# Eight experts on one core: TensorE's addresses in bytes, and the two copying engines in a loop of four turns

## The chip, the core and the metric

The kernel runs on one core of a Trainium2 chip. Its engines work side by side and meet only at semaphores: TensorE (PE in the profile, with its weight loads as PEld), VectorE (DVE), ScalarE (ACT), GpSimd (POOL) and SyncE (SP). The last two issue most of the transfers here, POOL on one queue and SP on another; sixteen DMA engines carry them out. The metric is the time of one execution on the device, in microseconds; lower is better.

## The reference

```python
n_experts, capacity, hidden, expert_hidden = 8, 256, 512, 2048
def reference(x, w1, w2):          # x [8,256,512], w1 [8,512,2048], w2 [8,2048,512], all float32
    h = np.matmul(x, w1)
    h = np.maximum(h, 0)
    return np.matmul(h, w2).astype(np.float32)
```

Each of the eight experts has its own x, w1 and w2. The weights are 8 x 2 x 4.19 MB, x and the result 4.19 MB each.

## The kernel before

**Transfers.** POOL loads the weights, one transfer per expert and layer (`load_w1`, L129; `load_w2`, L132), which turns float32 into bfloat16 on the way, so 4.19 MB are read and 2.10 MB written. There are two buffers for w1 (the halves of `w1_sb`) and two for w2 (`w2_sb`), used by even and odd experts. The order on POOL is fixed: the second half of x (`x_c`, L140), w1 of experts 0 and 1, a unit matrix, w2 of 0 and 1, and then for each further pair the two w1 and the two w2 (L156 to L162). Before a w1, POOL waits until TensorE is through layer 1 of the expert that had the buffer (`s_h`, L158); before a w2, until TensorE is through layer 2 of that expert (`s_o`, L161). w2 of the last expert comes in two pieces, 9 and 7 sixteenths (`CUT`, L137 and L138). Behind all loads POOL issues the results of experts 0 to 3 as one transfer (L164). SP loads the first half of x (`x_f`, L90) and at the end issues the results of experts 4 to 6 (L124) and 7 (L126).

**Tokens.** In between SP serves as TensorE's usher: it waits for each load, in the order in which TensorE needs them, and raises `t_w` (L114, L119, L121, L122), which TensorE takes down again. Ahead of the second expert of a pair it also waits until the first one's result has left `pt_o` (L117, `copied`).

**x.** The tokens have to be transposed. ScalarE and VectorE each run four rounds of `take_x` (L180), one for odd and one for even experts (in the last two rounds, for halves of the rows that four experts share): `cast` (L170, the copy at L175) writes the tile `x_b` in bfloat16, TensorE transposes it in eight blocks (L243), and a copy (L191 or L194) takes it from `pt_tr` to `xe`.

**The layers.** TensorE runs a loop over four pairs of experts (L246). Layer 1 of both experts (L247): in four turns of 16 matmuls, half of each turn into `pt_h0`, half into `pt_h1`; it takes the weights with a step of 16 columns. VectorE applies the relu to every `pt_h0` (L224), ScalarE to every `pt_h1` (L207), both into `ht_sb`; `t_hb` and `t_ha` give the halves back. Then layer 2 of both experts (L268): 32 matmuls into the two halves of `pt_o`, in groups (`GRP`). ScalarE copies the whole of `pt_o` to `out_sb` for experts 0 to 5 (L211); for experts 6 and 7 (`SOLO`) ScalarE and VectorE copy a half each (L214, L228). TensorE's loops address their operands through registers; `ahead` (L232) works the addresses out before the matmuls that use them, in elements of the tile. ScalarE's and VectorE's instructions are written out for all eight experts.

Of the kernel before, what the change touches and what calls it, by code (L numbers as in the profile page):

```python
# [9 lines left out]
def kernel(  # L10
# [7 lines left out]
    nc = tc.nc  # L18
    P = 128
    bf = mybir.dt.bfloat16  # L20
    f32 = mybir.dt.float32
    relu = mybir.ActivationFunctionType.Relu

    E, C, H = x.shape
    F = w1.shape[2]
    MT = C // P
    KT1 = H // P
    KT2 = F // P
    FB = 4
    NQ = KT2 // FB  # L30
    G = E // 2
    CUT = 9
    GRP = {0: 2, 2: 4, 6: 5, 11: 5}
    SOLO = E - 2

    w1_r = w1.rearrange("e (p kt) n -> e p kt n", p=P)
    w2_r = w2.rearrange("e (p kt) n -> e p kt n", p=P)
# [10 lines left out]
    x_c = nc.alloc_sbuf_tensor("x_c", [P, J, H], bf)  # L48
    x_b = nc.alloc_sbuf_tensor("x_b", [P, 2, KT1 * MT, P], bf)
    xe = nc.alloc_sbuf_tensor("xe", [P, E * KT1 * C], bf)  # L50
    w1_sb = nc.alloc_sbuf_tensor("w1_sb", [P, 2 * KT1 * F], bf)
    w2_sb = nc.alloc_sbuf_tensor("w2_sb", [P, 2 * KT2 * H], bf)
    ht = nc.alloc_sbuf_tensor("ht_sb", [P, 2 * KT2, H], bf)
    ht_f = ht[:].rearrange("p k n -> p (k n)")
    w1_k = w1_sb[:].rearrange("p (k n) -> p k n", n=F)
    w2_k = w2_sb[:].rearrange("p (k n) -> p k n", n=H)
    o_sb = nc.alloc_sbuf_tensor("out_sb", [P, E, MT, H], f32)
    identity = nc.alloc_sbuf_tensor("identity", [P, P], bf)
    ph = [nc.alloc_psum_tensor(f"pt_h{b}", [P, FB // 2, C], f32) for b in range(2)]
    po = nc.alloc_psum_tensor("pt_o", [P, MT, H], f32)  # L60
    pt = [nc.alloc_psum_tensor(f"pt_tr{b}", [P, KT1 * MT, P], bf) for b in range(2)]

    sem = nc.alloc_semaphore
# [2 lines left out]
    s_out = [sem(f"s_out{i}") for i in range(3)]  # L66
    s_w1 = [sem(f"s_w1_{e}") for e in range(E)]
    s_w2 = [sem(f"s_w2_{e}") for e in range(E)]
    s_w2b = sem("s_w2b")
    s_id = sem("s_id")  # L70
    s_act = sem("s_act")
    s_dve = sem("s_dve")
    s_tr = sem("s_tr")
    s_h = sem("s_h")
    s_o = sem("s_o")
    t_xb = sem("t_xb")
    s_xe = [sem(f"s_xe{b}") for b in range(2)]
    t_w = sem("t_w")
    t_ha = sem("t_ha")
    t_hb = sem("t_hb")  # L80

    sp, pool, act, dve, pe = nc.sync, nc.gpsimd, nc.scalar, nc.vector, nc.tensor

    def take(s, n=1):
        pe.wait_ge(s, n).then_inc(s, -n)  # L85
# [11 lines left out]

    def copied(eng, n):
        eng.wait_ge(s_act, n)
        if n > SOLO:  # L100
            eng.wait_ge(s_dve, n - SOLO)


    for e in range(G // 2, G):
# [1 line left out]
    for e in range(0, E, 2):  # L106
        for b in range(2):

            if e < G:
                sp.wait_ge(s_xe[b], e // 2 + 1)  # L110
            elif e + b == G:
                for s in s_xe:
                    sp.wait_ge(s, G)
            sp.wait_ge(s_w1[e + b], 16).then_inc(t_w, 1)  # L114
        for b in range(2):
            if b:
                copied(sp, e + 1)  # L117
            if e + b < E - 1:
                sp.wait_ge(s_w2[e + b], 16).then_inc(t_w, 2)  # L119
            else:  # L120
                sp.wait_ge(s_w2[e + b], 16).then_inc(t_w, 1)  # L121
                sp.wait_ge(s_w2b, 16).then_inc(t_w, 1)  # L122
    copied(sp, E - 1)
    sp.dma_start(out_r[:, G:E - 1], o_sb[:, G:E - 1]).then_inc(s_out[1], 16)  # L124
    copied(sp, E)
    sp.dma_start(out_r[:, E - 1], o_sb[:, E - 1]).then_inc(s_out[2], 16)  # L126


    def load_w1(e):  # L129
        pool.dma_start(w1_k[:, e % 2 * KT1:(e % 2 + 1) * KT1], w1_r[e]).then_inc(s_w1[e], 16)  # L130

    def load_w2(e):  # L132
        k = e % 2 * KT2
        if e < E - 1:
            pool.dma_start(w2_k[:, k:k + KT2], w2_r[e]).then_inc(s_w2[e], 16)  # L135
        else:
            pool.dma_start(w2_k[:, k:k + CUT], w2_r[e, :, :CUT]).then_inc(s_w2[e], 16)  # L137
            pool.dma_start(w2_k[:, k + CUT:k + KT2], w2_r[e, :, CUT:]).then_inc(s_w2b, 16)  # L138

    pool.dma_start(x_c[:], x_rows).then_inc(s_xc, 16)  # L140
    load_w1(0)
# [10 lines left out]
        channel_multiplier=1,  # L152
    ).then_inc(s_id, 1)
    load_w2(0)
    load_w2(1)
    for e in range(2, E, 2):  # L156
        for b in range(2):
            pool.wait_ge(s_h, 2 * NQ * (e + b - 1))  # L158
            load_w1(e + b)
        for b in range(2):  # L160
            pool.wait_ge(s_o, MT * (e + b - 1))  # L161
            load_w2(e + b)  # L162
    copied(pool, G)
    pool.dma_start(out_r[:, :G], o_sb[:, :G]).then_inc(s_out[0], 16)  # L164
# [5 lines left out]
    def cast(eng, r, b):  # L170

        a = 2 * r + b
        src = x_f[:, a] if a < G else x_c[:, MT * (a - G):MT * (a - G + 1)]
        copy = act.copy if eng is act else dve.tensor_copy
        copy(  # L175
            x_b[:, b].rearrange("p (t m) q -> p m q t", m=MT),
            src.rearrange("p m (q t) -> p m q t", t=KT1),
        ).then_inc(t_xb, 1)

    def take_x(eng, b):  # L180
# [16 lines left out]
                ).then_inc(s_xe[b], 1)  # L197


    act.sem_inc(t_ha, 1)  # L200
    take_x(act, 1)
    for e in range(0, E, 2):
        for b in range(2):
            for q in range(NQ):
                act.wait_ge(s_h, 2 * (NQ * (e + b) + q) + 2)
                k = KT2 * b + FB * q + FB // 2
                act.activation(ht[:, k:k + FB // 2, :C], ph[1][:], relu).then_inc(t_ha, 1)  # L207
        for b in range(2):
            if e + b < SOLO:
                act.wait_ge(s_o, MT * (e + b + 1))  # L210
                act.copy(o_sb[:, e + b], po[:]).then_inc(s_act, 1)  # L211
            else:
                act.wait_ge(s_o, MT * (e + b) + 2)
                act.copy(o_sb[:, e + b, 1], po[:, 1]).then_inc(s_act, 1)  # L214


    dve.sem_inc(t_hb, 1)
    take_x(dve, 0)
    for e in range(0, E, 2):
        for b in range(2):  # L220
            for q in range(NQ):
                dve.wait_ge(s_h, 2 * (NQ * (e + b) + q) + 1)
                k = KT2 * b + FB * q
                dve.tensor_relu(ht[:, k:k + FB // 2, :C], ph[0][:]).then_inc(t_hb, 1)  # L224
        for b in range(2):
            if e + b >= SOLO:
                dve.wait_ge(s_o, MT * (e + b) + 1)
                dve.tensor_copy(o_sb[:, e + b, 0], po[:, 0]).then_inc(s_dve, 1)  # L228

    def ahead(flat, weights, first, places, n, step=1):  # L232
        aps = [flat[:, bass.ds(first + k, n, step=step)] for k in places]
        for ap in aps:
            pe.lower_ap(ap, for_matmul_weights=weights)
        return aps

    pe.wait_ge(s_id, 2)
    with pe.Fori(0, G) as _r:
        take(t_xb, 2)  # L240
        for b in range(2):
            for j in range(KT1 * MT):
                ins = pe.transpose(pt[b][:, j], x_b[:, b, j], identity[:])  # L243
            ins.then_inc(s_tr, 1)

    with pe.Fori(0, G) as g:  # L246
        with pe.Fori(0, 2) as b:  # L247
            xs = ahead(xe, False, (g * 2 + b) * (KT1 * C), [kt * C for kt in range(KT1)], C)
            take(t_w)
            with pe.Fori(0, NQ) as q:  # L250
                for i in range(FB):
                    if i % 2 == 0:
                        ws = ahead(
                            w1_sb, True, b * (KT1 * F) + q * FB,
                            [kt * F + i + j for j in range(2) for kt in range(KT1)], P, KT2,
                        )
                        take((t_hb, t_ha)[i // 2])
                    for kt in range(KT1):
                        ins = pe.matmul(  # L259
                            ph[i // 2][:, i % 2, :],  # L260
                            ws[i % 2 * KT1 + kt],
                            xs[kt],
                            start=(kt == 0),
                            stop=(kt == KT1 - 1),
                        )
                    if i % 2:
                        ins.then_inc(s_h, 1)
        with pe.Fori(0, 2) as b:  # L268
            for kt in range(KT2):
                if kt in GRP:  # L270
                    k0, ks = kt, range(kt, kt + GRP[kt])
                    ws = ahead(w2_sb, False, b * (KT2 * H), [k * H for k in ks], H)
                    hs = ahead(
                        ht_f, True, b * (KT2 * H), [k * H + m * P for k in ks for m in range(MT)], P
                    )
                if kt == 3 * FB:
                    pe.wait_ge(t_hb, 1)
                if kt in (0, CUT):
                    take(t_w)
                for m in range(MT):  # L280
                    ins = pe.matmul(  # L281
                        po[:, m],
                        hs[(kt - k0) * MT + m],
                        ws[kt - k0],
                        start=(kt == 0),
                        stop=(kt == KT2 - 1),
                    )
                    if kt == KT2 - 1:
                        ins.then_inc(s_o, 1)

    for s in s_out:
        sp.wait_ge(s, 16)
# [30 lines left out]
```

## Time and profile before

| | us |
|---|---|
| three runs: lowest, median, highest | 180.07, 180.76, 182.46 |
| the profiled execution | 180.42 |
| its span, from the first to the last instruction | 178.8 |
| busy: PE, PEld | 126.0, 87.1 |
| busy: ACT, DVE, POOL | 54.1, 40.9, 14.3 |
| 15 of the loads of weights, median from issue to landing | 25.1 |

The span is what the views of the profile show; the 1.6 us between it and the execution's time lie around it. A group's row reads: line, engine, operation, output from input, shapes, count, then busy time, mean nanoseconds of one, idle time of the engine just ahead of them and what ended it. A row of the timeline begins with the start and the length in us; the bracket is the idle time before. "issue" and "PEq" stand for the engine's own instruction stream. SPq is SP's queue. A row of stretches has the stretch, its length, each engine's busy time with the count, the clock granted to TensorE, the DMA engines' busy share and the GB/s that they wrote.

### The profile page before, as it was taken

The numbers are of one execution on the slowest core, as the hardware profiler recorded it, in microseconds if no ns is written. First come the engines' busy times: TensorE is split into PE (matmuls) and PEld (weight loads), VectorE is DVE, ScalarE is ACT, GpSimd is POOL, SyncE is SP. The second block draws the span as 40 slices with busy tenths as digits, with TensorE's granted clock in tenths as the row PEclk, the third lists the DMA queues.
The fourth block names the chain that finished last, engine by engine and source line by source line (L and its number), as shares of the span: only waits on it lengthen the run. The fifth ranks groups of instructions, "written<-read, shape, count | busy, mean of one in ns | idle before, by whom it ended". The sixth has DMA issues, their size and how long they took to land. (4 is left out here: it accounts for less than half of the span.)

```text
span 178.8 us, 2547 instructions
## 1 busy us (share of the span) xinstructions
PE 126.0 (70%) x824; PEld 87.1 (49%) x832; DVE 40.9 (23%) x42; ACT 54.1 (30%) x49; POOL 14.3 (8%) x25
## 2 busy tenths in 40 slices
PE   0040403099799979979997997989495695989880
PEld 0030303078786335868642486864142585854330
DVE  0725527263231000323200033330000132310110
ACT  2759596952222021322202042220202121310110
POOL 3920000000101010010101011010103000000000
PEclk9999999999999999999999999999999999999997
DMA  5999999999998998998999999899899899999898
GB/s 194 361 207 235 231 194 220 231 213 202 231 231 183 235 227 183 235 231 187 227 231 198 216 231 227 187 231 231 183 235 231 180 235 231 198 203 221 253 420 351
DMA packets 4240, 40.90 MB, mean 229 GB/s; under 512 B 400, under 2 KB 400, under 8 KB 2064
## 3 DMA queue, kind: packets, MB, share of 16 engines
q0 software_dynamic: 3120, 36.70, 94.2%
q1 hardware_dynamic: 1120, 4.19, 5.9%
HBM read 71.30 MB, written 4.19 MB: 422 GB/s over the span
## 5 line engine op out<-in xcount | busy, mean ns | idle before, releaser
L259 PE MATMUL pt_h<-xe,w_sb 128*128 x512 | 62.9, 277 | 9.6 <-PEq L85 8.7
L259 PEld LDWEIGHTS pt_h<-xe,w_sb 128*128 x512 | 56.2, 146 | 16.8 <-issue 16.1
L281 PE MATMUL pt_o<-w_sb,ht_sb 128*128 x248 | 56.1, 379 | 7.9 <-PEq L85 6.2
L224 DVE TENSOR_SCALAR ht_sb<-pt_h 128x512 bf16<-128x512 f32 x32 | 22.1, 692 | 96.3 <-PE pt_h L259 96.3
L281 PEld LDWEIGHTS pt_o<-w_sb,ht_sb 128*128 x256 | 24.4, 97 | 38.3 <-issue 11.2
L207 ACT ACTIVATE ht_sb<-pt_h 128x512 bf16<-128x512 f32 x32 | 19.1, 597 | 49.9 <-PE pt_h L259 49.9
L243 PE MATMUL pt_tr<-identity,x_b 128*128 128x128 bf16 x64 | 7.5, 310 | 30.1 <-PEq L85 30.1
L243 PEld LDWEIGHTS pt_tr<-identity,x_b 128*128 128x128 bf16 x64 | 6.5, 144 | 30.8 <-issue 30.8
L211 ACT COPY out_sb<-pt_o 128x1024 f32<-128x1024 f32 x6 | 6.1, 1015 | 43.2 <-PE pt_o L281 43.2
L175 ACT CAST x_b<-x_f 128x1024 bf16<-128x1024 f32 x2 | 10.4, 5189 | 1.3 <-DMA x_f<-in_x_dram 1.3
L130 POOL DMA_DIRECT2D w_sb<-in_w_dram x8 | 4.3, 535 | 76.3 <-PE pt_h L259 76.3
L175 ACT COPY x_b<-x_c 128x1024 bf16<-128x1024 bf16 x2 | 9.5, 4774 | 0.0
L175 DVE CAST x_b<-x_f 128x1024 bf16<-128x1024 f32 x2 | 6.1, 3040 | 5.5 <-DMA x_f<-in_x_dram 5.5
L194 DVE COPY xe<-pt_tr 128x1024 bf16<-128x1024 bf16 x2 | 4.9, 2457 | 8.5 <-PE pt_tr L243 8.5
L135 POOL DMA_DIRECT2D w_sb<-in_w_dram x7 | 3.7, 533 | 35.7 <-PE pt_o L281 35.7
L194 ACT COPY xe<-pt_tr 128x1024 bf16<-128x1024 bf16 x2 | 5.0, 2494 | 4.1 <-PE pt_tr L243 4.1
L214 ACT COPY out_sb<-pt_o 128x512 f32<-128x512 f32 x2 | 1.2, 586 | 14.6 <-PE pt_o L281 14.6
L175 DVE COPY x_b<-x_c 128x1024 bf16<-128x1024 bf16 x2 | 5.4, 2676 | 0.0
L228 DVE COPY out_sb<-pt_o 128x512 f32<-128x512 f32 x2 | 1.4, 692 | 15.0 <-PE pt_o L281 15.0
L145 POOL TENSOR_SCALAR_AFFINE_SELECT identity<-identity 128x128 bf16<-128x128 bf16 x1 | 3.5, 3491 | 0.2 <-POOL identity L143 0.2
L191 ACT COPY xe<-pt_tr 128x1024 bf16<-128x1024 bf16 x2 | 2.0, 1012 | 4.1 <-PE pt_tr L243 4.1
L191 DVE COPY xe<-pt_tr 128x1024 bf16<-128x1024 bf16 x2 | 1.4, 692 | 7.8 <-PE pt_tr L243 7.8
(10 smaller groups left out, 4.4 us busy)
## 6 DMA issues: line engine op xcount, KB each, us to landing
w_sb<-in_w_dram POOLq DMA_DIRECT2D x15, 2048.0 KB, 25.1
x_f<-in_x_dram SPq DMA_DIRECT2D x4, 512.0 KB, 4.0
out_dram<-out_sb POOLq DMA_DIRECT2D x1, 2048.0 KB, 36.7
out_dram<-out_sb SPq DMA_DIRECT2D x1, 1536.0 KB, 8.6
w_sb<-in_w_dram POOLq DMA_DIRECT2D x1, 1152.0 KB, 27.0
x_c<-in_x_dram POOLq DMA_DIRECT2D x1, 1024.0 KB, 9.9
w_sb<-in_w_dram POOLq DMA_DIRECT2D x1, 896.0 KB, 31.1
out_dram<-out_sb SPq DMA_DIRECT2D x1, 512.0 KB, 4.5
```

What stands on the lines that cost most here:

```text
L130: pool.dma_start(w1_k[:, e % 2 * KT1:(e % 2 + 1) * KT1], w1_r[e]).then_inc(s_w1[e], 16)
L135: pool.dma_start(w2_k[:, k:k + KT2], w2_r[e]).then_inc(s_w2[e], 16)
L145: pool.affine_select(out=identity[:], in_=identity[:], compare_op=mybir.AluOpType.not_equal, fill=1.0, base=0, pattern=[[-1, P]], channel_ ...
L175: copy(x_b[:, b].rearrange("p (t m) q -> p m q t", m=MT), src.rearrange("p m (q t) -> p m q t", t=KT1),).then_inc(t_xb, 1)
L191: copy(xe[:, a * n:(a + 1) * n], pt[b][:].rearrange("p j q -> p (j q)")).then_inc(s_xe[b], 1)
L194: copy(xl[:, :, :, :, a - G].rearrange("p l j q -> p j l q"), pt[b][:].rearrange("p j (l q) -> p j l q", l=G),).then_inc(s_xe[b], 1)
L207: act.activation(ht[:, k:k + FB // 2, :C], ph[1][:], relu).then_inc(t_ha, 1)
L211: act.copy(o_sb[:, e + b], po[:]).then_inc(s_act, 1)
L224: dve.tensor_relu(ht[:, k:k + FB // 2, :C], ph[0][:]).then_inc(t_hb, 1)
L243: ins = pe.transpose(pt[b][:, j], x_b[:, b, j], identity[:])
L259: ins = pe.matmul(ph[i // 2][:, i % 2, :], ws[i % 2 * KT1 + kt], xs[kt], start=(kt == 0), stop=(kt == KT1 - 1),)
L281: ins = pe.matmul(po[:, m], hs[(kt - k0) * MT + m], ws[kt - k0], start=(kt == 0), stop=(kt == KT2 - 1),)
```

## The change

Nothing in the arithmetic changes. The parts:

- `ahead` views its tile as bytes, so that the loop counters are multiplied out to byte offsets; `w1_sb` becomes 16 elements (32 bytes) longer, since the strided views now end later.
- ScalarE and VectorE go through the layers in a loop of four turns, one for each pair (`layers`). Each has semaphores of its own for the relus (`s_ha`, `s_hb`) and for the results (`s_oa`, `s_ob`), which it counts down at the end of a turn. Each copies its half of every result.
- `copied` therefore waits for both engines, for every expert. POOL waits for ScalarE's relus (`s_first`) and for ScalarE's copies (`s_act`) in place of TensorE's matmuls.
- w2 of expert 6 comes in two pieces as well.
- `cast` keeps its source and target and goes through them in another order.

```diff
-    w1_sb = nc.alloc_sbuf_tensor("w1_sb", [P, 2 * KT1 * F], bf)
+    w1_sb = nc.alloc_sbuf_tensor("w1_sb", [P, 2 * KT1 * F + KT2], bf)
...
     def copied(eng, n):
         eng.wait_ge(s_act, n)
-        if n > SOLO:
-            eng.wait_ge(s_dve, n - SOLO)
+        eng.wait_ge(s_dve, n)
...
-            if e + b < E - 1:
+            if e + b < E - 2:
                 sp.wait_ge(s_w2[e + b], 16).then_inc(t_w, 2)
             else:
                 sp.wait_ge(s_w2[e + b], 16).then_inc(t_w, 1)
-                sp.wait_ge(s_w2b, 16).then_inc(t_w, 1)
+                sp.wait_ge(s_w2b[b], 16).then_inc(t_w, 1)
...
-        if e < E - 1:
+        if e < E - 2:
             pool.dma_start(w2_k[:, k:k + KT2], w2_r[e]).then_inc(s_w2[e], 16)
...
-            pool.wait_ge(s_h, 2 * NQ * (e + b - 1))
+            pool.wait_ge(s_first, e + b - 1)
             load_w1(e + b)
         for b in range(2):
-            pool.wait_ge(s_o, MT * (e + b - 1))
+            pool.wait_ge(s_act, e + b - 1)
             load_w2(e + b)
...
         copy(
-            x_b[:, b].rearrange("p (t m) q -> p m q t", m=MT),
-            src.rearrange("p m (q t) -> p m q t", t=KT1),
+            x_b[:, b].rearrange("p (t m) q -> p t m q", m=MT),
+            src.rearrange("p m (q t) -> p t m q", t=KT1),
         ).then_inc(t_xb, 1)
...
+    def layers(eng, half, s_h, s_o, t_h, s_copied):
+        by = o_sb[:].rearrange("p e m n -> p (e m n)").bitcast(mybir.dt.uint8)
+        with eng.Fori(0, G) as g:
+            outs = []
+            for b in range(2):
+                n = H * 4
+                outs.append(by[:, bass.ds(g * (2 * MT * n) + (MT * b + half) * n, n)].bitcast(f32))
+                eng.lower_ap(outs[b])
+            for b in range(2):
+                for q in range(NQ):
+                    k = KT2 * b + FB * q + FB // 2 * half
+                    dst, i = ht[:, k:k + FB // 2, :C], NQ * b + q + 1
+                    eng.wait_ge(s_h, i)
+                    if eng is act:
+                        act.activation(dst, ph[half][:], relu).then_inc(t_h, 1)
+                    else:
+                        dve.tensor_relu(dst, ph[half][:]).then_inc(t_h, 1)
+                if eng is act:
+                    act.sem_inc(s_first, 1)
+            eng.wait_ge(s_h, 2 * NQ).then_inc(s_h, -2 * NQ)
+            for b in range(2):
+                eng.wait_ge(s_o, b + 1)
+                copy = act.copy if eng is act else dve.tensor_copy
+                copy(outs[b], po[:, half]).then_inc(s_copied, 1)
+            eng.wait_ge(s_o, 2).then_inc(s_o, -2)
...
     def ahead(flat, weights, first, places, n, step=1):
-        aps = [flat[:, bass.ds(first + k, n, step=step)] for k in places]
-        for ap in aps:
-            pe.lower_ap(ap, for_matmul_weights=weights)
+        by = flat[:].bitcast(mybir.dt.uint8)
+        aps = []
+        for k in places:
+            ap = by[:, bass.ds(first + 2 * k, 2 * n * step)].bitcast(bf)
+            aps.append(ap if step == 1 else ap.rearrange("p (n s) -> p n s", s=step)[:, :, 0])
+            pe.lower_ap(aps[-1], for_matmul_weights=weights)
         return aps
...
-                        ins.then_inc(s_h, 1)
+                        ins.then_inc((s_hb, s_ha)[i // 2], 1)
...
-                        ins.then_inc(s_o, 1)
+                        ins.then_inc((s_ob, s_oa)[m], 1)
```

More of the change, by code (lines that the diff above doesn't have):

```diff
@@ L33 @@
     GRP = {0: 2, 2: 4, 6: 5, 11: 5}
-    SOLO = E - 2
     w1_r = w1.rearrange("e (p kt) n -> e p kt n", p=P)
@@ L54 @@
     ht_f = ht[:].rearrange("p k n -> p (k n)")
-    w1_k = w1_sb[:].rearrange("p (k n) -> p k n", n=F)
+    w1_k = w1_sb[:, :2 * KT1 * F].rearrange("p (k n) -> p k n", n=F)
     w2_k = w2_sb[:].rearrange("p (k n) -> p k n", n=H)
@@ L68 @@
     s_w2 = [sem(f"s_w2_{e}") for e in range(E)]
-    s_w2b = sem("s_w2b")
+    s_w2b = [sem(f"s_w2b_{e}") for e in range(E - 2, E)]
     s_id = sem("s_id")
@@ L73 @@
     s_tr = sem("s_tr")
-    s_h = sem("s_h")
-    s_o = sem("s_o")
+    s_ha = sem("s_ha")
+    s_hb = sem("s_hb")
+    s_first = sem("s_first")
+    s_oa = sem("s_oa")
+    s_ob = sem("s_ob")
     t_xb = sem("t_xb")
@@ L137, in load_w2 @@
             pool.dma_start(w2_k[:, k:k + CUT], w2_r[e, :, :CUT]).then_inc(s_w2[e], 16)
-            pool.dma_start(w2_k[:, k + CUT:k + KT2], w2_r[e, :, CUT:]).then_inc(s_w2b, 16)
+            pool.dma_start(w2_k[:, k + CUT:k + KT2], w2_r[e, :, CUT:]).then_inc(s_w2b[e - E], 16)
     pool.dma_start(x_c[:], x_rows).then_inc(s_xc, 16)
@@ L200 @@
     act.sem_inc(t_ha, 1)
     take_x(act, 1)
[L202 to L214, printed above, removed]
+    layers(act, 1, s_ha, s_oa, t_ha, s_act)
@@ L217 @@
     dve.sem_inc(t_hb, 1)
     take_x(dve, 0)
[L219 to L228, printed above, removed]
@@ L232, in ahead @@
-    def ahead(flat, weights, first, places, n, step=1):
-        aps = [flat[:, bass.ds(first + k, n, step=step)] for k in places]
-        for ap in aps:
-            pe.lower_ap(ap, for_matmul_weights=weights)
+    layers(dve, 0, s_hb, s_ob, t_hb, s_dve)
+    def ahead(flat, weights, first, places, n, step=1):
+        by = flat[:].bitcast(mybir.dt.uint8)
[4 more added lines that the diff above has]
+            pe.lower_ap(aps[-1], for_matmul_weights=weights)
@@ L247 @@
         with pe.Fori(0, 2) as b:
-            xs = ahead(xe, False, (g * 2 + b) * (KT1 * C), [kt * C for kt in range(KT1)], C)
+            xs = ahead(xe, False, g * (4 * KT1 * C) + b * (2 * KT1 * C), [kt * C for kt in range(KT1)], C)
             take(t_w)
@@ L253 @@
                         ws = ahead(
-                            w1_sb, True, b * (KT1 * F) + q * FB,
+                            w1_sb, True, b * (2 * KT1 * F) + q * (2 * FB),
                             [kt * F + i + j for j in range(2) for kt in range(KT1)], P, KT2,
@@ L271 @@
                     k0, ks = kt, range(kt, kt + GRP[kt])
[L272 to L275, printed above, removed]
+                    ws = ahead(w2_sb, False, b * (2 * KT2 * H), [k * H for k in ks], H)
+                    hs = ahead(ht_f, True, b * (2 * KT2 * H), [k * H + m * P for k in ks for m in range(MT)], P)
                 if kt == 3 * FB:
```

## The prediction

> **What bounds the kernel now.** I read the page's first four parts, then the waits of SyncE's queue, then stretches of the span, then the timeline. TensorE looks like the bound: busy 70%, and the chain that ended last is made of its lines. The second part and the queues say something else.
>
> ```profile
> PE 126.0 (70%) x824; PEld 87.1 (49%) x832; DVE 40.9 (23%) x42; ACT 54.1 (30%) x49; POOL 14.3 (8%) x25
> ...
> DMA  5999999999998998998999999899899899999898
> ...
> HBM read 71.30 MB, written 4.19 MB: 422 GB/s over the span
> ...
> PE pt_o L281 4%; ACT out_sb L214 0%
> ```
>
> The DMA row is 8 or 9 in every slice but the first. A finer cut:
>
> ```profile
> 0.00:2.00 2.00, 0.00 (x0) 0.00 (x0) 0.00 (x0) 0.00 (x0) 0.20 (x4) 1.00 0.00 0
> 2.00:8.00 6.00, 0.00 (x0) 0.00 (x0) 2.48 (x1) 3.77 (x2) 4.43 (x5) 1.00 1.00 371
> 8.00:23.00 15.00, 3.73 (x32) 3.25 (x32) 7.16 (x5) 10.91 (x5) 2.04 (x3) 1.00 1.03 219
> 23.00:100.00 77.00, 60.67 (x401) 42.81 (x406) 18.79 (x20) 25.68 (x23) 3.70 (x7) 1.00 1.02 218
> 100.00:168.00 68.00, 56.03 (x369) 38.73 (x370) 11.76 (x17) 13.19 (x20) 3.92 (x7) 1.00 1.01 212
> 168.00:178.00 10.00, 5.53 (x25) 2.33 (x24) 0.69 (x1) 0.59 (x1) 0.00 (x0) 0.91 1.01 416
> 178.00:178.80 0.80, 0.00 (x0) 0.00 (x0) 0.00 (x0) 0.00 (x0) 0.00 (x0) 0.50 0.08 31
> ```
>
> The last two columns are the DMA engines' share and the GB/s written. From 2.0 to 178.0 us the share is 1.00 or more; only the first 2.0 and the last 0.8 us are empty. The weights are read as float32 and written as bfloat16, so 218 GB/s written is 436 read. SyncE waits for each weight transfer and then runs one semaphore instruction, whose start shows when the transfer was there (count, durations, first to last start):
>
> ```profile
> L114 SPq EVENT_SEMAPHORE  x8: 17/28/28, 22.9 to 148.8; - x8
> ...
> L119 SPq EVENT_SEMAPHORE  x7: 17/17/11573, 42.3 to 158.5; - x7
> ...
> L122 SPq EVENT_SEMAPHORE  x1: 17/17/17, 168.7 to 168.7; - x1
> ```
>
> w1 of expert 0 is there at 22.9 and w1 of expert 7, thirteen transfers later in the order of issue, at 148.8: 9.68 us each. From w2 of expert 0 to w2 of expert 6 twelve take 116.2 us: 9.68 again. A transfer reads 4.19 MB (512 x 2048 x 4), so 433 GB/s, without a gap. **The bound is this stream**: 75.5 MB between 2.0 and 178.0 us. TensorE does not set its pace:
>
> ```profile
> 70.62 7.86 PE L259 MATMUL pt_h<-xe,w_sb 128*128 x64
> ...
> 102.47 7.85 PE L259 MATMUL pt_h<-xe,w_sb 128*128 x64
> ...
> 140.29 7.85 PE L259 MATMUL pt_h<-xe,w_sb 128*128 x64 [3.57 <-PEq L85]
> 149.93 7.88 PE L259 MATMUL pt_h<-xe,w_sb 128*128 x64 [1.79 <-PEq L85]
> 158.66 7.07 PE L281 MATMUL pt_o<-w_sb,ht_sb 128*128 x31 [0.84 <-PEq L85]
> 166.52 7.07 PE L281 MATMUL pt_o<-w_sb,ht_sb 128*128 x31 [0.79 <-PEq L85]
> ```
>
> While it catches up, a pair of experts takes it 102.47 - 70.62 = 31.85 us; the stream needs 4 x 9.68 = 38.7. From about 120 us on it waits for weights. So TensorE work that goes is worth nothing unless it makes the stream start earlier, run without a gap where there was one, or end earlier; and work that comes costs nothing until the queue of transfers runs dry.
>
> [...]
>
> **Part by part.** *The way into layer 1.* The diff also turns the order in which L175 walks its tile: it wrote in steps of 512 bytes and now writes in sequence, reading every fourth element instead.
>
> ```profile
> L259 PEld LDWEIGHTS pt_h<-xe,w_sb 128*128 x512 | 56.2, 146 | 16.8 <-issue 16.1
> ...
> L281 PEld LDWEIGHTS pt_o<-w_sb,ht_sb 128*128 x256 | 24.4, 97 | 38.3 <-issue 11.2
> ...
> L175 ACT CAST x_b<-x_f 128x1024 bf16<-128x1024 f32 x2 | 10.4, 5189 | 1.3 <-DMA x_f<-in_x_dram 1.3
> L175 ACT COPY x_b<-x_c 128x1024 bf16<-128x1024 bf16 x2 | 9.5, 4774 | 0.0
> ...
> L191 ACT COPY xe<-pt_tr 128x1024 bf16<-128x1024 bf16 x2 | 2.0, 1012 | 4.1 <-PE pt_tr L243 4.1
> ```
>
> ScalarE's is the longer half of each of the four rounds. As many elements in sequence take it 1.01 us; the only strided read in the trace is TensorE's weight load at L259, 146 ns against 97 in sequence, half as much again. So I take 1.01 x 1.5 = 1.5 us, with 1.0 and 1.5 x 4.8 = 7.2 us as ends. That removes about 3.3 us per round, 13 in all, and layer 1 of expert 0 starts near 25 us instead of
>
> ```profile
> 37.88 8.74 PE L259 MATMUL pt_h<-xe,w_sb 128*128 x64 [0.29 <-PEq L85]
> ...
> 46.92 0.53 POOL L130 DMA_DIRECT2D w_sb<-in_w_dram  x1 [36.88 <-PE pt_h L259]
> ```
>
> but not before 22.9, when its weights are there. What does the end gain? Nothing: the four transfers queued at the start last until 42.3 + 9.68 = 52.0 us, and the next, w1 of expert 2, is issued at 46.92 already. Issued near 34, it lands at 61.7 all the same. What is late next is the stream itself.
>
> *TensorE's addresses.* In the built program TensorE holds 15 address instructions instead of 32.
>
> ```profile
> 142.22 1.74 PEld L259 LDWEIGHTS pt_h<-xe,w_sb 128*128 x16 [0.23 <-issue]
> ```
>
> A stretch of 64 matmuls at L259 takes 7.85 us in four turns, each with such a pause of 0.2 us between its weight loads and the last turn's, so at most 0.8 us per expert goes, and some of the 1.1 us between the weights' arrival (148.8) and the first matmul (149.93). Worst case nothing goes. All of it lies beside the stream.
>
> *The loops and the halves.*
>
> ```profile
> L224 DVE TENSOR_SCALAR ht_sb<-pt_h 128x512 bf16<-128x512 f32 x32 | 22.1, 692 | 96.3 <-PE pt_h L259 96.3
> ...
> L207 ACT ACTIVATE ht_sb<-pt_h 128x512 bf16<-128x512 f32 x32 | 19.1, 597 | 49.9 <-PE pt_h L259 49.9
> ...
> L211 ACT COPY out_sb<-pt_o 128x1024 f32<-128x1024 f32 x6 | 6.1, 1015 | 43.2 <-PE pt_o L281 43.2
> ...
> L228 DVE COPY out_sb<-pt_o 128x512 f32<-128x512 f32 x2 | 1.4, 692 | 15.0 <-PE pt_o L281 15.0
> ```
>
> Six copies of 1.015 us become halves of 0.59 (ScalarE, at the end of the timeline) and 0.69 us side by side: pt_o is free 0.3 us sooner, three times. In return VectorE has 0.69 us of copy ahead of the first relu of a pair, and a branch and two addresses per turn, not in the trace; zero to 1 us is my bound for them, from the 1.1 us that TensorE takes over its own loop heads and addresses. Behind a late relu stands TensorE, which needs the half of pt_h again 1.95 us (7.85 / 4) later; a pair has 38.7 - 31.85 = 6.8 us to spare. Cost nothing; without that cover up to 1 us four times.
>
> *Waits.* POOL issues w1 after ScalarE's last relu of the expert (up to 0.6 us later), w2 after the copy (up to 1). Behind the waiting POOL stand its other loads and the first output. The thinnest cover of the old order is the 52.0 - 46.92 = 5.1 us above; once TensorE lives from hand to mouth, a load is issued some 10 us after its predecessor's arrival, with two or three others still queued. Nothing. SyncE waits for VectorE's copy as well; L124 still stands behind the last piece of w2.
>
> *w2 of expert 6 in two pieces.* Layer 2 at 158.66 no longer waits for the whole (158.5): it starts when layer 1 ends, near 157.9, or 157 with the addresses. The piece itself costs between nothing and 0.5 us: for expert 7, already cut so, the two pieces took 168.7 - 158.5 = 10.2 us against 9.68. I take 0.1, because the outputs behind it fill the engines.
>
> *The end.*
>
> ```profile
> 173.62 0.59 ACT L214 COPY out_sb<-pt_o 128x512 f32<-128x512 f32 x1 [7.27 <-PE pt_o L281]
> 174.23 0.35 SPq L126 DMA_DIRECT2D out_dram<-out_sb  x1
> ```
>
> With layer 2 of expert 6 earlier, the last output is issued 0.8 to 2 us before 174.23, no earlier than 168.7 + 7/16 x 7.07 + 0.6 = 172.4. But from 168.7 on 4.19 MB of results are left, and at 416 GB/s they need 10.1 us: 178.8. The engines are full until 178.0, whatever their order. Gain at most the 0.8 us of the last stretch, taken as nothing.
>
> The whole move of w2, the hidden rows and the results by 32 bytes (w1_sb is 16 elements longer) has no row. [...]
>
> **Sum**, against the profiled 180.42 (span 178.8 and 1.62 around it): 0 + 0 + 0 + 0 + 0.1 + 0 = 180.5. The three runs shown, 180.07 to 182.46, have their median 0.34 above that; I say **180.6**.
>
> **Rivals.** (a) *The end is shorter*: the last output shares the engines sooner and 0.8 us go, 179.8. For it: share 0.08 after 178.0. Against it: a write must still land. (b) *Slower, the queue runs dry at w1 of expert 2*: if strided reading is dearer than strided writing, every round gets longer. Layer 1 may slip until the issue at 46.92 comes 5.1 us less the 2 us in which a new transfer shows nothing (as at 0 to 2), so by 3 us, 0.8 per round. At 7.2 us per cast, 2.4 more, it slips 9.6 and the stream stands still for 6.6: **187**. Against it: the old writes already step 512 bytes, the new reads 8 or 16. (c) *The shifted buffers slow their transfers*: eight loads and the results, 8 x 9.68 + 10.1 = 87.5 us, at the 416 of the last stretch against 433, 4%: 3.5 us, 183.9. [...] (d) *The addresses do not get shorter*, or the loops cost what they save: TensorE's stretches stay at 7.85, and the time too, 180.6; it changes the view, not the forecast.
>
> **How the numbers follow.** Forecast with (d) 0.86, (a) 0.05, (c) 0.04, (b) 0.03, something on the fast side that I do not see 0.02. Low end 179.7, (a) with a little scatter; high end 182.2, the forecast with the split's 0.5 and a scatter like that of the three runs (1.7 above their median, rarely of a median). Two per cent, 3.6 us, is about what a measurement of this kernel can tell from no change; all of the forecast and (a) lie within it, and half of (c). Faster by over 2% would need the stream to do 75.5 MB in 172.4 us, 438 GB/s: 0.02. Slower: (b), half of (c), and 0.01 for what I do not see: 0.06.
>
> **What would show it.** Right: share 1.00 from 2 to 178 us; w1 of expert 7 there near 148.8, the last piece of w2 near 168.8; layer 1 of expert 0 at 23 to 28 us; gaps of about 2 us ahead of each layer from then on; stretches at L259 shorter than 7.85. Wrong: a stretch with a share well under 1, first after 52 us (b); loads of w2 longer than 9.68 beside loads of w1 that are not (c); an end later than ten us after the last piece of w2.

## The result and the profile after

The changed kernel takes 180.34 us in the median of 20 runs (179.85 to 181.09), the kernel before 180.92 (180.07 to 182.46); the ratio is 0.9964, with a 95% interval of 0.9946 to 0.9981. That is 0.6 us less, far under 2%, and inside the predicted range of 179.7 to 182.2 around 180.6. The profiled execution took 179.85 us, its span 178.5.

Nearly everything inside the span moved, and its end did not. First the page, the lines that answer to those shown of before:

```profile
PE 130.2 (73%) x824; PEld 89.1 (50%) x832; DVE 37.2 (21%) x48; ACT 37.8 (21%) x49; POOL 12.6 (7%) x26
...
DMA  5999999989989989999999998999998999999998
...
HBM read 71.30 MB, written 4.19 MB: 423 GB/s over the span
...
PE pt_o L289 4%; ACT out_sb L225 0%
```

ScalarE lost 16 us of work, VectorE 4. TensorE's busy time even grew by 4 us. The DMA row is as full as it was, and so are the stretches (DMA share and GB/s written in the last two columns):

```profile
0.00:2.00 2.00, 0.00 (x0) 0.00 (x0) 0.00 (x0) 0.00 (x0) 0.20 (x4) 1.00 0.03 6
2.00:8.00 6.00, 0.38 (x4) 0.41 (x5) 1.09 (x1) 3.30 (x2) 4.18 (x7) 1.00 1.00 364
8.00:23.00 15.00, 6.23 (x56) 5.52 (x55) 6.00 (x6) 8.23 (x6) 0.00 (x0) 1.00 1.04 221
23.00:100.00 77.00, 63.57 (x388) 42.40 (x390) 16.32 (x21) 14.41 (x21) 4.25 (x8) 0.96 1.02 218
100.00:168.00 68.00, 56.03 (x363) 39.08 (x367) 13.15 (x19) 11.31 (x19) 3.93 (x7) 0.97 1.01 213
168.00:178.00 10.00, 4.01 (x18) 1.67 (x17) 0.69 (x1) 0.59 (x1) 0.00 (x0) 0.87 1.01 414
```

SyncE's semaphore instructions behind its waits for the loads (count, durations, first and last start):

```profile
L115 SPq EVENT_SEMAPHORE  x8: 17/28/28, 22.8 to 148.7; - x8
...
L120 SPq EVENT_SEMAPHORE  x6: 17/22/28, 42.3 to 129.4; - x6
...
L122 SPq EVENT_SEMAPHORE  x2: 17/39/61, 154.3 to 164.8; - x2
...
L123 SPq EVENT_SEMAPHORE  x2: 17/17/17, 158.5 to 168.5; - x2
```

w1 of expert 0 is there at 22.8 us, w1 of expert 7 at 148.7, the last piece of w2 at 168.5; before it was 22.9, 148.8 and 168.7. The stream runs at the same 9.68 us per load. TensorE's timeline is another one:

```profile
23.64 8.54 PE L269 MATMUL pt_h<-xe,w_sb 128*128 x64
33.27 7.78 PE L269 MATMUL pt_h<-xe,w_sb 128*128 x64 [1.08 <-PEq L87]
42.41 7.07 PE L289 MATMUL pt_o<-w_sb,ht_sb 128*128 x31 [1.37 <-PEq L87]
52.09 8.75 PE L289 MATMUL pt_o<-w_sb,ht_sb 128*128 x31 [2.61 <-PEq L87]
62.33 7.78 PE L269 MATMUL pt_h<-xe,w_sb 128*128 x64 [1.49 <-PEq L87]
72.05 9.17 PE L269 MATMUL pt_h<-xe,w_sb 128*128 x64 [1.95 <-PEq L87]
...
90.83 7.07 PE L289 MATMUL pt_o<-w_sb,ht_sb 128*128 x31 [2.61 <-PEq L87]
...
149.53 7.77 PE L269 MATMUL pt_h<-xe,w_sb 128*128 x64 [1.95 <-PEq L87]
157.13 7.07 PE L289 MATMUL pt_o<-w_sb,ht_sb 128*128 x31
164.99 7.07 PE L289 MATMUL pt_o<-w_sb,ht_sb 128*128 x31 [0.79 <-PEq L87]
```

Layer 1 of expert 0 starts 14 us earlier (37.88 before), and from then on TensorE waits for each load and then runs at once: most starts lie 0.1 to 0.9 us behind a load. Layer 2 of expert 6 starts 1.5 us earlier, right behind layer 1. The end of the timeline and the landing of the results (page, part 6):

```profile
171.88 0.69 DVE L225 COPY out_sb<-pt_o 128x512 f32 x1 [7.17 <-PE pt_o L289]
172.10 0.59 ACT L225 COPY out_sb<-pt_o 128x512 f32 x1 [7.27 <-PE pt_o L289]
172.71 0.35 SPq L127 DMA_DIRECT2D out_dram<-out_sb  x1
```

```profile
out_dram<-out_sb SPq DMA_DIRECT2D x1, 1536.0 KB, 8.6
...
out_dram<-out_sb SPq DMA_DIRECT2D x1, 512.0 KB, 5.8
```

The last result is issued 1.5 us sooner and takes 1.3 us longer to land (5.8 against 4.5): it stands in the same full engines (share 1.01 from 168 to 178 us). So 179.85 - 178.5 = 1.35 us lie around the span, where it was 180.42 - 178.8 = 1.62. This small term, which the prediction took as fixed, turns out to hold the gain; one execution of each kernel could not show it, the experiments do.

### The profile page after: what moved, and what is told of

It is laid out like the page before. It is cut to its first block, busy times and chain, and to the rows that moved or that the text cites. A ratio compares the mean times of both kernels' runs of the same rounds, so it can differ in the third digit from the quotient of the medians.

```text
span 178.5 us, 2361 instructions
## 1 busy us (share of the span) xinstructions
PE 130.2 (73%) x824; PEld 89.1 (50%) x832; DVE 37.2 (21%) x48; ACT 37.8 (21%) x49; POOL 12.6 (7%) x26
## 5 line engine op out<-in xcount | busy, mean ns | idle before, releaser
L269 PE MATMUL pt_h<-xe,w_sb 128*128 x512 | 65.4, 285 | 13.7 <-PEq L87 13.6
L269 PEld LDWEIGHTS pt_h<-xe,w_sb 128*128 x512 | 57.6, 147 | 22.0 <-issue 20.0
L289 PE MATMUL pt_o<-w_sb,ht_sb 128*128 x248 | 57.8, 387 | 11.8 <-PEq L87 11.4
L225 DVE COPY out_sb<-pt_o 128x512 f32 x8 | 5.5, 692 | 66.5 <-PE pt_o L289 66.5
L225 ACT COPY out_sb<-pt_o 128x512 f32 x8 | 4.7, 586 | 64.6 <-PE pt_o L289 64.6
L131 POOL DMA_DIRECT2D w_sb<-in_w_dram x8 | 4.3, 534 | 70.9 <-ACTq L220 70.9
L136 POOL DMA_DIRECT2D w_sb<-in_w_dram x6 | 3.2, 536 | 35.5 <-ACT out_sb L225 35.5
L176 ACT CAST x_b<-x_f 128x1024 bf16<-128x1024 f32 x2 | 4.0, 2008 | 1.3 <-DMA x_f<-in_x_dram 1.3
L176 DVE CAST x_b<-x_f 128x1024 bf16<-128x1024 f32 x2 | 2.2, 1079 | 6.0 <-DMA x_f<-in_x_dram 6.0
L138 POOL DMA_DIRECT2D w_sb<-in_w_dram x2 | 1.1, 531 | 17.1 <-ACT out_sb L225 17.1
L176 ACT COPY x_b<-x_c 128x1024 bf16<-128x1024 bf16 x2 | 2.2, 1119 | 0.0
L176 DVE COPY x_b<-x_c 128x1024 bf16<-128x1024 bf16 x2 | 1.4, 696 | 0.0
```

The costliest lines, as they stand in the source:

```text
L176: copy(x_b[:, b].rearrange("p (t m) q -> p t m q", m=MT), src.rearrange("p m (q t) -> p t m q", t=KT1),).then_inc(t_xb, 1)
L225: copy(outs[b], po[:, half]).then_inc(s_copied, 1)
L269: ins = pe.matmul(ph[i // 2][:, i % 2, :], ws[i % 2 * KT1 + kt], xs[kt], start=(kt == 0), stop=(kt == KT1 - 1),)
L289: ins = pe.matmul(po[:, m], hs[(kt - k0) * MT + m], ws[kt - k0], start=(kt == 0), stop=(kt == KT2 - 1),)
```

## The experiments

Two questions: is the stream of transfers really what sets the end, with the deciding point that the prediction gave for its rival (b); and where do the 0.6 us come from? The expectations give their explanations names in capitals. STREAM and TENSORE say that the transfers, or TensorE's chain, set the end. END, FRONT and REST put the gain on the earlier last result, on the earlier start of layer 1, or on TensorE's shorter address work; OUTSIDE, which came later, puts it on the length of ScalarE's and VectorE's programs. "The rest" in small letters is a run's time less its own span. Names: "the kernel before" and "the changed kernel" as above; each ratio is to the kernel before on the same chip.

### Starving the queue by a known amount

```diff
-            pool.wait_ge(s_h, 2 * NQ * (e + b - 1))
+            pool.wait_ge(s_h, 12 if e + b == 2 else 2 * NQ * (e + b - 1))
```

> The kernel before, with w1 of expert 2 issued only after half of layer 1 of expert 1: at about 51.6 us instead of 46.9. The four loads in hand last until 52.0. STREAM, by the prediction's rule (3 us are free, then 1 us per us): the slip of 4.7 us costs 1.7 us, 182.6. TENSORE (TensorE's chain sets the end, it has time to spare): no cost, 180.9.

The same edit with 16 in place of 12:

> The same with w1 of expert 2 issued after the whole of layer 1 of expert 1, at about 55.6 us, a slip of 8.7 us. STREAM: 5.7 us, 186.6, and a stretch with an empty DMA share from 52 to near 57 us; the difference to the run before is 4 us. TENSORE: below 2 us, since TensorE only catches up later in the stream.

Measured: 182.67 us (two runs, 182.40 and 182.94) and 186.71 (185.80 and 187.61), where the kernel before took 180.56 (median of 9). The second one's stretches and POOL's timeline show the hole:

```profile
50.00:52.00 2.00, 1.91 (x18) 1.70 (x17) 0.66 (x2) 0.60 (x1) 0.00 (x0) 1.00 0.62 131
52.00:54.00 2.00, 2.00 (x19) 1.79 (x18) 0.75 (x2) 0.60 (x1) 0.00 (x0) 1.00 0.00 0
54.00:56.00 2.00, 2.00 (x13) 1.04 (x12) 0.33 (x1) 0.60 (x1) 1.06 (x2) 1.00 0.00 0
56.00:58.00 2.00, 2.00 (x11) 0.88 (x9) 0.00 (x0) 0.00 (x0) 0.00 (x0) 1.00 1.09 164
```

```profile
54.77 1.06 POOL L130 DMA_DIRECT2D w_sb<-in_w_dram  x2 [45.69 <-PE pt_h L259]
```

While TensorE works on, the DMA share is 0.00 for four microseconds, and the hole is handed on to the end: the span is 184.1 us, and 180.7 with 12. The loads were issued at 54.77 and 51.41 us, slips of 7.85 and 4.49 against 46.92; the spans grew by 5.3 and 1.9 over 178.8. So 2.6 us are free at both points, and what goes beyond is paid one for one. That rests on one profiled execution of each kernel; the other run with 16 took 1.8 us longer, with a span of 186.0, so the 2.6 may be off by a microsecond or more. The rule had 3 us free, from a start-up of 2 us. That its times came out within 0.1 us of the medians of two runs is in part luck: the issues were earlier than I had put them. TENSORE, which expected no cost with 12 and under 2 us with 16, is refuted.

### Half of TensorE's work in layer 1

```diff
-                    for kt in range(KT1):
+                    for kt in range(KT1 // 2):
...
-                            stop=(kt == KT1 - 1),
+                            stop=(kt == KT1 // 2 - 1),
```

> The changed kernel with half of layer 1's matmuls left out (two of the four blocks of the hidden dimension). TensorE loses about 31 us of busy time. STREAM: 180.3, the same within 0.5 us. TENSORE: several us less.

Measured: 180.05 us (8 runs), ratio 0.9963 (0.992 to 1.0007), the changed kernel's own. Half of 512 matmuls can go without a trace in the time. TensorE's busy time fell only from 130.2 to 114.6 us, half of the 31 expected; the clock granted in the profiled execution was 0.90, against 0.96 in the changed kernel's.

### Four megabytes less

```diff
+        n = KT1 if e < E - 2 else KT1 // 2
-        pool.dma_start(w1_k[:, e % 2 * KT1:(e % 2 + 1) * KT1], w1_r[e]).then_inc(s_w1[e], 16)
+        pool.dma_start(w1_k[:, e % 2 * KT1:e % 2 * KT1 + n], w1_r[e, :, :n]).then_inc(s_w1[e], 16)
```

> The changed kernel with only half of w1 loaded for experts 6 and 7 (the other half of the buffer keeps the weights of experts 4 and 5, so these two experts' results differ). 4.19 MB less to read, all else alike. STREAM: 9.7 us less, 170.7. TENSORE: layer 1 of expert 6 starts 4.8 us earlier, but its matmuls are all there; at most 3 us less.

Measured: 174.12 us (174.00 and 174.25), 6.2 less than the changed kernel, neither 9.7 nor "at most 3"; both expectations missed. The stream did end earlier; then something else was last. Stretches of that run, TensorE's timeline, and the landing of its last result:

```profile
160.00:165.00 5.00, 4.21 (x20) 1.79 (x19) 0.69 (x1) 0.59 (x1) 0.00 (x0) 1.00 1.00 406
165.00:170.00 5.00, 4.51 (x21) 1.86 (x19) 0.61 (x1) 0.40 (x1) 0.00 (x0) 1.00 0.47 188
```

```profile
130.17 8.75 PE L290 MATMUL pt_o<-w_sb,ht_sb 128*128 x31 [2.61 <-PEq L87]
138.76 7.74 PE L270 MATMUL pt_h<-xe,w_sb 128*128 x64
147.03 7.77 PE L270 MATMUL pt_h<-xe,w_sb 128*128 x64 [0.53 <-PEq L87]
```

```profile
out_dram<-out_sb SPq DMA_DIRECT2D x1, 512.0 KB, 2.7
```

The last w1 was there at 139.7 and the first piece of w2 of expert 6 at 145.2, well ahead of 147.03 and 154.64, when TensorE came to them. So from 138.76 on TensorE runs without a wait for a load, and the DMA share falls to 0.47 behind 165 us: for the first time the engines stand idle before the end. The last result lands 2.7 us after its issue when it has the engines nearly to itself. By that price TensorE's chain would have ended at 174.23 + 2.7 = 176.9 in the kernel before and at 172.71 + 2.7 = 175.4 in the changed one (estimates), 1.9 and 3.1 us ahead of the ends that were seen, 178.8 and 178.5. So the stream is the bound, but with only about 3 us of cover over TensorE in the changed kernel. The profiled span fell by 178.5 - 172.9 = 5.6 us: these 3.1, and 2.5 more because TensorE's chain itself moved up from 175.4 to 172.9, its weights for layer 1 of experts 6 and 7 being there sooner. The change widened the cover by 1.2 us, which is worth nothing as long as the bytes stay.

### Where the 0.6 us come from: one part at a time

w2 of expert 6 in two pieces alone, in the kernel before (`b_split`; the semaphore of the second piece is left out here), and taken back in the changed one (`a_whole`):

```diff
-            if e + b < E - 1:
+            if e + b < E - 2:
                 sp.wait_ge(s_w2[e + b], 16).then_inc(t_w, 2)
...
-        if e < E - 1:
+        if e < E - 2:
             pool.dma_start(w2_k[:, k:k + KT2], w2_r[e]).then_inc(s_w2[e], 16)
```

> The kernel before with w2 of expert 6 in two pieces and nothing else of the change. The change as a whole is worth 0.6 us (0.9964). END (the last result is issued earlier and shares the engines sooner): layer 2 of expert 6 starts near 157.9 instead of 158.66, the last output is issued near 173.4, and most of the gain is here: 180.5, ratio 0.997 to 0.998. FRONT (the casts give it): no gain, ratio 1.000. REST (shorter address work): ratio 1.000.

> The changed kernel with w2 of expert 6 in one piece again. END: the last output goes back to about 173.9 and most of the gain is lost, ratio to the kernel before 0.999. FRONT and REST: the gain stays, ratio 0.996 to 0.997.

The new order of the casts alone (`b_cast`), and the old order in the changed kernel (`a_oldcast`):

```diff
-            x_b[:, b].rearrange("p (t m) q -> p m q t", m=MT),
-            src.rearrange("p m (q t) -> p m q t", t=KT1),
+            x_b[:, b].rearrange("p (t m) q -> p t m q", m=MT),
+            src.rearrange("p m (q t) -> p t m q", t=KT1),
```

> The kernel before with the casts' new order alone. Layer 1 of expert 0 starts near 23.6 instead of 37.9 and w1 of expert 2 is issued near 33. STREAM with END: no gain, ratio 1.000, for the queue of loads never ran dry. FRONT: ratio 0.996 to 0.997.

> The changed kernel with the casts in the old order. Layer 1 of expert 0 starts near 37.9 again, 14 us later. STREAM with END: nothing is lost, ratio to the kernel before 0.996 to 0.997; TensorE's idle gaps from 40 to 110 us close up. FRONT: the gain goes, ratio 1.000.

Measured (12 runs each): `b_split` 180.41, ratio 0.9969 (0.9941 to 0.9997); `a_whole` 180.37, 0.9957 (0.9929 to 0.9986); `b_cast` 181.06, 1.0013 (0.9984 to 1.0043); `a_oldcast` 180.21, 0.9957 (0.9932 to 0.9982). FRONT is refuted by both sides: the casts move 14 us of TensorE's start (layer 1 begins at 23.64 in the changed kernel, at 37.41 in `a_oldcast`) and none of the time. END met its ratio in `b_split`, but not its path: in the profiled execution layer 2 of expert 6 started at 159.56 and the last result was issued at 175.13, later than before, where 157.9 and 173.4 were expected. And without the split the changed kernel keeps its whole gain, though its last result is issued as late as before, at

```profile
174.33 0.35 SPq L127 DMA_DIRECT2D out_dram<-out_sb  x1
```

What did tell the kernels apart was the rest, the part of each run's time that lies around its span: 1.3 us in the changed kernel and its two variants, 1.6 to 1.7 in most runs of the kernel before and its two. (Not "in every run without", as the next expectation has it: some had 2.5 us and more.) Three more kernels asked which part does that: the loops written out with fixed addresses, all else as changed (`a_flat`),

```diff
-        with eng.Fori(0, G) as g:
+        for g in range(G):
...
-                outs.append(by[:, bass.ds(g * (2 * MT * n) + (MT * b + half) * n, n)].bitcast(f32))
-                eng.lower_ap(outs[b])
+                at = g * (2 * MT * n) + (MT * b + half) * n
+                outs.append(by[:, at:at + n].bitcast(f32))
```

> The changed kernel with the loops of ScalarE and VectorE written out again (fixed addresses, four turns one after the other), all else as changed. Around the span 1.31 to 1.35 us were left in every run with the loops, 1.62 to 1.70 in every run without. OUTSIDE (the length of ScalarE's and VectorE's programs costs 0.3 us around the span): the rest goes back to 1.6 or 1.7 us, ratio to the kernel before 0.998. REST (shorter address work in TensorE): the rest stays near 1.3, ratio 0.996.

the function `layers` with its semaphores in the kernel before, without byte addresses, new casts or split (`b_loops`), and the byte addresses alone, with the longer `w1_sb` that they need (`b_bytes`):

```diff
...
-        aps = [flat[:, bass.ds(first + k, n, step=step)] for k in places]
-        for ap in aps:
-            pe.lower_ap(ap, for_matmul_weights=weights)
+        by = flat[:].bitcast(mybir.dt.uint8)
+        aps = []
+        for k in places:
+            ap = by[:, bass.ds(first + 2 * k, 2 * n * step)].bitcast(bf)
+            aps.append(ap if step == 1 else ap.rearrange("p (n s) -> p n s", s=step)[:, :, 0])
+            pe.lower_ap(aps[-1], for_matmul_weights=weights)
...
```

> The kernel before with the loops and the halves alone: element addresses, the old casts, w2 of expert 6 in one piece. OUTSIDE: the rest around the span falls to 1.3 us, ratio 0.997 to 0.998, and the span stays 178.8. REST: the rest stays 1.65, ratio 1.000.

> The kernel before with TensorE's byte addresses alone. Stretches of 64 matmuls of layer 1 take 7.77 instead of 7.86 us. OUTSIDE: the rest stays 1.65 us, ratio 0.999 to 1.000. REST: the rest falls to 1.3, ratio 0.996 to 0.998.

and last the halves alone (`b_halves`):

```diff
-    SOLO = E - 2
+    SOLO = 0
```

> The kernel before with halves alone: ScalarE and VectorE copy a half of every result, everything is written out, and the semaphores count up as before. So far the rest around the span has its median at 1.66 us for the kernel before, 1.49 with byte addresses alone, 1.50 with loops, halves and new semaphores alone, 1.31 with all of it and also with all of it written out. HALVES: rest 1.50, no runs above 2 us, ratio 0.997 to 0.999. SEMAPHORES (the counting down, or the new waits): rest 1.66, some runs above 2 us, ratio 1.000. The span's median stays within 178.8 to 179.2 by both.

Measured: `a_flat` 180.52, ratio 0.9979 (0.9952 to 1.0005); `b_loops` 180.62, 0.9972 (0.9946 to 0.9998); `b_bytes` 180.56, 0.9984 (0.9959 to 1.0008); `b_halves` 181.85, 1.0053 (1.0025 to 1.0081). `b_bytes` and `b_loops` came out, by their rests, halfway between their two expectations, `b_halves` by neither of its two. The single runs' spans and times, put together (medians over all runs; the 89 of the kernel before are those run beside the experiments, since for the 20 of the result no spans are on record):

| kernel | runs | span | rest | runs with a rest over 1.9 us |
|---|---|---|---|---|
| before | 89 | 179.0 | 1.66 | 17 (2.5 to 3.1) |
| `b_split` | 12 | 178.8 | 1.65 | 1 |
| `b_cast` | 12 | 179.0 | 1.68 | 5 |
| `b_halves` | 12 | 178.9 | 2.91 | 11 |
| `b_bytes` | 12 | 179.1 | 1.49 | 0 |
| `b_loops` | 12 | 179.1 | 1.50 | 0 |
| `a_flat` | 12 | 179.2 | 1.31 | 0 |
| `a_whole` | 12 | 179.1 | 1.32 | 0 |
| `a_oldcast` | 12 | 178.9 | 1.32 | 0 |
| changed | 20 | 179.0 | 1.31 | 0 |

The medians of the spans lie within 0.4 us of each other, and before and after the change they are the same, 179.0. **The gain is all in the rest**: 0.35 us in the median, and the long rests of the kernel before, 2.5 to 3.1 us in nearly a fifth of its runs, are gone from the changed kernel and its variants. The byte addresses, with the longer `w1_sb`, take 0.17 us off it, `layers` alone 0.16; in each the longest of 12 rests, 1.55 and 1.53, is below the shortest of the kernel before, 1.59. The two were not run together without the other parts of the change, but the changed kernel has 1.31, and 1.32 without the split and without the new casts. It is not the loop: written out in the changed kernel, the rest is 1.31 too, so OUTSIDE as I had put it (the length of the programs) fell. The number of instructions executed does not order the rest either: 2547 before, 2299 in `b_bytes` and 2607 in `b_loops`, whose rests are alike, and 2361 in the changed kernel. Nor do the halves do it alone: in the kernel before they lengthen the rest by 1.25 us, more than the whole loss of `b_halves`, 1.0 us, while its span stays. What else `layers` brings are its semaphores and waits; they were not tried by themselves, nor was the longer `w1_sb`, and the parts may act on each other. What happens in the rest no row of the profile shows. So it is shown where the gain lies and which parts of the change bring it, but why they shorten the rest, and why the halves alone lengthen it, stays open. Open too is whether the split is worth something: `b_split` has a span 0.2 us shorter and fewer long rests than the kernel before, which 12 runs don't settle.

## Why the prediction was right, point by point

- **The bound.** Right: share 1.00 or more from 2 to 178 us, 9.68 us per load, and shown from both sides, by the starved queue and by the halved matmuls. The 1.9 to 3.1 us by which TensorE's chain ends ahead of the stream were not worked out; they limit what a shorter stream alone would bring.
- **The way into layer 1.** Direction and worth (nothing) were right. ScalarE's casts take 2.01 us from float32 and 1.12 from bfloat16 where the estimate was 1.5 for both:

```profile
L176 ACT CAST x_b<-x_f 128x1024 bf16<-128x1024 f32 x2 | 4.0, 2008 | 1.3 <-DMA x_f<-in_x_dram 1.3
...
L176 ACT COPY x_b<-x_c 128x1024 bf16<-128x1024 bf16 x2 | 2.2, 1119 | 0.0
```

  The mean was about right, but by luck. The factor of 1.5 came from weight loads with a step (146 ns) against others in sequence (97 ns), called the only strided read in the trace. In the page of before, the loads for the transposes, of whole blocks in sequence, take 144 ns too, so these rows don't show the price of a step:

```profile
L243 PEld LDWEIGHTS pt_tr<-identity,x_b 128*128 128x128 bf16 x64 | 6.5, 144 | 30.8 <-issue 30.8
```

  The start at 23.64 lies between the floor of 22.9 and the 25 that were forecast.
- **TensorE's addresses.** Of the "at most 0.8 us" per stretch 0.1 went (7.77 against 7.86), and the lag behind the load fell from 1.1 to 149.53 - 148.7 = 0.8. The pause of 0.2 us between turns is still there, so fewer address instructions don't shorten it.
- **Loops, halves and waits.** Right at nothing within the span (what they bring lies in the rest): w1 of expert 2 was issued at 32.53 (forecast: near 34), and the queue never came near its end.
- **The split.** 0.1 fits: the two pieces of expert 6 are there 158.5 - 148.7 = 9.8 us after the load before them, against 9.7 in one piece, one execution each. Layer 2 starts at 157.13, the forecast's 157.
- **The end, and rival (a).** The last output left at 172.71, within the 172.4 to 173.4 given, and the span did not follow: its median is 179.0 as before. Rival (a) fell.
- **Rival (b)** did not come, but its price was about right: 2.6 us are free, by one execution at each of two points, where it had 3. **Rival (c)** fell: from w2 of expert 0 (there at 42.3) to w2 of expert 5 (129.4) nine loads, five of them into the moved buffer, take the same 9.68 us each, and the results leave at 414 GB/s against 416. No run shows a price of the 32 bytes. Rival (d) fell in part: the stretches did get shorter, by little.
- **The sum.** The term that failed is "1.62 around it": it was held constant without a reason, and measures 1.31 in the median of the changed kernel. So the forecast of no change to the span was right, and the small gain that came had no term in the sum.
- **Luck.** That 180.34 lies so near to 180.6 is in part chance. The sum gave 180.5 for the profiled execution; the median of the three runs lay 0.34 above that execution's 180.42, and only 0.1 of this went into the forecast, without a reason. With all of it the forecast is 180.9, and from the 180.92 of 20 runs it is 181.0: still inside the range, but 0.5 to 0.7 us above what came.

## What to carry to other kernels

Before a change to the engines is priced, look whether the transfers run without a gap and when the queue would run dry: here 14 us at the front, 16 us of ScalarE's time and half of layer 1's matmuls were all worth nothing, while a load issued 4.5 us later cost 2. Compare the other chain as well, with the price of its last step when it is alone, since it limits what a shorter stream brings. And for differences of a few tenths of a microsecond, compare the span and the time around it separately; a gain need not lie where the diff works.

## What the runs showed of the hardware that was not expected

TensorE's granted clock fell behind some of its waits for loads, and not behind others. The gap of 2.61 us ahead of 52.09 was followed by a stretch of 8.75 us instead of 7.07, and the clock (the last column but two) reads

```profile
50.00:52.00 2.00, 0.00 (x0) 0.00 (x0) 0.00 (x0) 0.10 (x1) 0.53 (x1) 1.00 1.08 229
52.00:56.00 4.00, 3.92 (x11) 1.49 (x12) 0.00 (x0) 0.00 (x0) 0.00 (x0) 0.57 0.98 209
56.00:60.00 4.00, 3.95 (x19) 1.77 (x19) 0.00 (x0) 0.00 (x0) 0.00 (x0) 1.00 1.15 246
```

Over that whole stretch it was 0.80. Behind the same gap ahead of 90.83 the stretch took 7.07 us at 1.00, so the length of the gap alone does not decide it. Two stretches of layer 1, at 72.05 and 101.11, took 9.17 and 8.84 us instead of 7.77, at 0.81 and 0.85; with the one at 52.09 that is 4.2 us, as much as TensorE's busy time grew. With the new casts alone the clock is lower too: over the runs its mean was 0.986 in the kernel before and 0.966 in `b_cast`. It cost nothing here, the spans have the same median of 179.0 us; in the run with fewer bytes one such stretch (130.17, 8.75 us; the clock was 0.83 from 130 to 140 us) lies on the chain that ended last.

GpSimd's own work takes longer beside VectorE's first cast, though no semaphore stands between the two; so it is not only at semaphores that engines meet here. In the kernel before the unit matrix took 3.49 us beside a cast of 3.35 us, with the new order 1.19 us beside 1.09; in the run with w1 latest (`b_late16`), where GpSimd came first, it took 0.28 us, and the next two transfers were issued in 3.15 us instead of 1.08:

```profile
5.52 0.28 POOL L145 TENSOR_SCALAR_AFFINE_SELECT identity<-identity 128x128 bf16<-128x128 bf16 x1 [0.24 <-POOL identity L143]
5.55 2.88 DVE L175 CAST x_b<-x_f 128x1024 bf16<-128x1024 f32 x1 [5.55 <-DMA x_f<-in_x_dram]
5.93 3.15 POOL L135 DMA_DIRECT2D w_sb<-in_w_dram  x2
```

Six profiles show both rows. In three (`b_late16`, `a_less`, `b_halves`) GpSimd's work on the unit matrix begins ahead of the cast and takes 0.28 us; the issue that follows takes 3.15, 1.45 and 3.44 us and ends 0.65 to 0.67 us after the cast. In the other three (the kernel before, the changed one, `a_oldcast`) the cast begins first or with it; the unit matrix takes 3.49, 1.19 and 3.50 us and ends 0.14 to 0.16 us after the cast. What holds GpSimd up no row shows. It delays nothing here: w2 of expert 0 is there 19.4 us behind w1 of expert 0 in the kernel before (42.3 and 22.9), 19.5 in the changed one and 19.4 in `b_late16`, which is two loads of 9.68 us.
